# FFN weights in a two-layer hybrid block: down weights in quarters with slots of their own, up weights in turns over two pairs

## The chip, the cores and the metric

The kernel runs on one core of one Trainium2 chip. The metric is the device time of one execution in microseconds (us), the median of several runs; a lower one is better. The trace is one profiled execution of the same program. Engines are named PE (matrix products; PEld its weight loads), DVE, ACT, POOL and SP (SP issues nearly all transfers here).

## What is computed

A backbone of two layers over 1280 tokens (1024 latent and 256 context tokens) of 1024 features. Each layer has three groups of mixers (attention, mLSTM, Hyena), a shared output projection, and then the ConvFFN that this case is about; conditioning (adaLN) gives shift, scale and gate of each norm. The last layer needs only the 1024 latent tokens. The ConvFFN in the reference's terms, cut to what matters:

```python
D_FF = ((8 * D_MODEL // 3 + 255) // 256) * 256      # 2816
# u = norm2(x) @ w_up                 -> 2 * D_FF features: a half "a" and a half "b"
# u = dwconv(u, 3 taps along tokens)  -> each feature by itself
# g = silu(a) * b
# x = x + gate * (g @ w_down)         -> 1024 features
```

Products are wanted at fp32 accuracy, and the kernel makes each from three products of fp32r halves (hi by hi, hi by lo, lo by hi).

## The kernel before

**Tiles.** Features lie on the 128 partitions, tokens along the free axis, in blocks of 512, 512 and 256 tokens (the last layer has the first two only). The 2816 hidden features are 22 tiles. For one tile j and one half `ab` (0 for a, 1 for b) `up` computes `u`: 8 input tiles by 3 passes by the blocks, so 72 matmuls in layer 0 and 48 in layer 1, into the PSUM tile `u3` (printed as `u`). `conv` then takes `u` through ACT (L1525), DVE (L1526, L1527) and for ab = 0 ACT again (L1530); DVE multiplies the halves (L1551); `split` makes `g` hi on ACT (L290) and lo on DVE (L291).

**Pairs.** Tiles come in pairs (2p, 2p+1), 11 of them. The loop of `ffn` runs up of the even tile, then `down` of the pair before, then up of the odd tile. Below, ua0 and ub0 are the two up weights of the even tile, ua1 and ub1 those of the odd one. `down` makes, for each of 8 tiles of output features and each block, one piece: 6 matmuls (two j by three passes) into the PSUM tile `pj` or `pk` in turn, one buffer each, and DVE's L1576 adds the piece, times the gate, onto the residual stream `S`. A piece can so only start when L1576 has emptied the piece two before it. The down of the last pair stands behind the loop, with the blocks outermost, and feeds the next norm.

**Weights.** A raw weight tile `wr` (128x1024 fp32, 512 KB, two slots) comes by a transfer on SP's queue: one for each up weight (L295), one for each half of the output features of a pair's down weights (L1562). `wsplit` makes hi from it by an ACT cast (L307) and lo by a POOL subtraction (L308). The raw slot is free when both are through; the slots of hi and lo are free when the last matmul that reads them is through. In the FFN these 1024-wide slots are three pairs: two named `wh` and one named `wx`, which all weights, up and down, take in turn:

```python
self.wturn = (self.wturn + 1) % 3
if self.wturn == 0:
    p, tag = self.wx, "wx"
```

**Order.** A list scheduler of the framework gives each engine its order when the program is built, from dependences, slots and its own estimates; the engines then run their lists in order and wait for each other by semaphores. So the order of engines is known beforehand, and the rows of the section on the change are taken from it. SP's list too is in order: a transfer that waits for a slot holds all behind it.

**What else runs.** In layer 0 DVE also computes the adaLN rows of layer 1 in between (`ada_some`, L416, printed as CUSTOM_DVE_ANT_0 in the trace and as ISA in the order, each with a read of its accumulator behind it), 12 for each tile j, with weights `aw` that SP loads into three slots (L412).

Of the kernel before, what the change touches and what calls it, by code (L numbers as in the profile page):

```python
# [196 lines left out]
class Kern:  # L197
    def __init__(self, tc, a, out):
        self.tc, self.nc, self.a, self.out = tc, tc.nc, a, out
        self.n = self.turn = self.wturn = 0  # L200
        self.wx = self.adas = None
        self.wpool = False
        self.pools, self.fixed, self.events = [], 0, 0

# [90 lines left out]
        self.nc.sync.dma_start(wr[:, :cols], ap)  # L295
        return self.wsplit(wr[:, :cols], cols)

    def wsplit(self, wr, cols=1024):

        p, tag = self.wp, "wh"  # L300
        if self.wx is not None:
            self.wturn = (self.wturn + 1) % 3
            if self.wturn == 0:
                p, tag = self.wx, "wx"
        hi = self.t(p, [128, 1024], tag, F32R)[:, :cols]
        lo = self.t(p, [128, 1024], tag, F32R)[:, :cols]
        self.nc.scalar.copy(hi, wr)  # L307
        (self.nc.gpsimd if self.wpool else self.nc.vector).tensor_tensor(lo, wr, hi, op=ALU.subtract)  # L308
        return hi, lo
# [1191 lines left out]
    def ffn(self, L, xs, hs, rp, pp, between):  # L1501

        nc, a = self.nc, self.a
        last = L == DEPTH - 1
        blocks = [0, 1] if last else [0, 1, 2]
        W = 1024 if last else TP
        ffc = self.t(rp, [128, 44, 4], "ffc")
        nc.sync.dma_start(ffc, a["ffc"][L])

        def begin(j, ab):  # L1510
            return [j, ab, self.weight(a["wup"][L, j, ab]), self.t(pp, [128, 1024 if last else 1536], "u3")]

        def piece(u, b):
            wh, wl = u[2]
            t0 = BLK[b][0]
            for k in range(8):
                hi, lo = hs[k][b]
                self.mm3(u[3][:, t0:t0 + hi.shape[-1]], wh[:, 128 * k:128 * k + 128], wl[:, 128 * k:128 * k + 128],
                         hi, lo, k == 0, k == 7)

        def conv(u):
            j, ab, _, pu = u
            cw = ffc[:, j + N_FF * ab]
            y = self.t(rp, [128, TP], "sa")
            nc.scalar.activation(y[:, :W], pu[:, :W], AF.Identity, scale=cw[:, 1:2], bias=cw[:, 3:4])  # L1525
            nc.vector.scalar_tensor_tensor(y[:, 1:W], pu[:, 0:W - 1], cw[:, 0:1], y[:, 1:W], op0=ALU.mult, op1=ALU.add)  # L1526
            nc.vector.scalar_tensor_tensor(y[:, 0:W - 1], pu[:, 1:W], cw[:, 2:3], y[:, 0:W - 1], op0=ALU.mult, op1=ALU.add)  # L1527
            self.ada_some(pu, 3)
            if ab == 0:
                nc.scalar.activation(y[:, :W], y[:, :W], AF.Silu)  # L1530
            return y

        def up(j):
            if j == 0:
                us = [begin(j, ab) for ab in range(2)]
                for u in us:
                    piece(u, 0)
                ys = []
                for u in us:
                    for b in blocks[1:]:  # L1540
                        piece(u, b)
                    ys.append(conv(u))
            else:
                ys = []
                for ab in range(2):
                    u = begin(j, ab)
                    for b in blocks:
                        piece(u, b)
                    ys.append(conv(u))
            ya, yb = ys  # L1550
            nc.vector.tensor_tensor(yb[:, :W], ya[:, :W], yb[:, :W], op=ALU.mult)  # L1551
            self.ada_some(ya, 3)
            gh = self.t(rp, [128, TP], "g", F32R)
            gl = self.t(rp, [128, TP], "g", F32R)
            self.split(yb[:, :W], gh[:, :W], gl[:, :W])
            self.ada_some(yb, 3)
            return gh, gl

        def down_w(js, mh):

            wr = self.t(self.wp, [128, 1024], "wr")
            nc.sync.dma_start(wr.rearrange("p (j c) -> p j c", j=2),  # L1562
                              a["wdn"][L, js[0]:js[0] + 2, :, 512 * mh:512 * mh + 512].rearrange("j p c -> p j c"))
            hi, lo = self.wsplit(wr)
            return [(hi[:, 512 * i:512 * i + 512], lo[:, 512 * i:512 * i + 512]) for i in range(2)]

        def down_piece(gs, ws, m, b):
            t0, n, s = BLK[b]
            h0 = t0 + s
            ps = self.ps()[:, :n]  # L1570
            for i, ((gh, gl), (wh, wl)) in enumerate(zip(gs, ws)):
                o = 128 * (m % 4)
                self.mm3(ps, wh[:, o:o + 128], wl[:, o:o + 128], gh[:, h0:h0 + n], gl[:, h0:h0 + n],
                         i == 0, i == len(gs) - 1)
            x = xs[m][:, t0:t0 + n]
            nc.vector.scalar_tensor_tensor(x, ps, self.mods[L][:, 40 + m, s:s + 1], x, op0=ALU.mult, op1=ALU.add)  # L1576

        def down(js, gs):
            for mh in range(2):
                ws = down_w(js, mh)  # L1580
                for m in range(4 * mh, 4 * mh + 4):
                    for b in blocks:
                        down_piece(gs, ws, m, b)

        pend = None
        for p in range(N_FF // 2):
            g0 = up(2 * p)
            if pend is not None:
                down(*pend)
            g1 = up(2 * p + 1)  # L1590
            pend = ((2 * p, 2 * p + 1), (g0, g1))
        js, gs = pend
        accs = {}
        assert self.adas is None
        if not last:
            self.gain(L + 1, 0)
            self.gain(L + 1, 1, 1)
        self.wpool = WP
        for b in blocks:
            for mh in range(2):  # L1600
                ws = down_w(js, mh)
                for m in range(4 * mh, 4 * mh + 4):
                    down_piece(gs, ws, m, b)
                    accs[b] = self.square(accs.get(b), xs[m], b, rp, ("B", "B"), nc.gpsimd if BETA and b < 2 else None)
                    if m == MB and b:
                        between(b - 1, accs[b - 1])
        between(blocks[-1], accs[blocks[-1]])
        self.wpool = False
# [11 lines left out]
    def run(self):  # L1620
        nc, a = self.nc, self.a
        with ExitStack() as es:
# [46 lines left out]
            for L in range(DEPTH):  # L1669
# [22 lines left out]
                        assert self.adas is None  # L1692
                        self.gain(L, 1)
                with ExitStack() as e4:
                    rp = self.pool(e4, f"r5{L}", sa=2, g=6, wx=2, aw=3, rs_s=1, rs_r=1, rs_v=1, rs_d=1)
                    src = a["xT"] if L == 0 else self.xsp
                    nt = NX if last else T
                    xs = []
# [13 lines left out]
                    self.w_out(L, xs, groups, between_w)  # L1712
                    for b in groups[-1]:
                        norm2(b)
                    self.wx = rp
                    pp = self.pool(e4, f"p5{L}", PSUM, u3=3 if last else 2)
                    if not last:
                        self.hs = [{} for _ in range(8)]
# [15 lines left out]
                        self.ada_run(chain(self.ada_rows(1, range(16), (0, 1), *args),  # L1734
                                           self.ada_rows(1, range(16, 48), (0,), *args)))
                    self.ffn(L, xs, hs, rp, pp, between)
                    self.wx = None


# [15 lines left out]
```

## Time and profile before

| what | value |
|---|---|
| median of 3 runs | 3794.49 us (3793.99 to 3797.38) |
| profiled execution, its own time | 3789.71 us |
| its span in the trace | 3787.9 us |
| TensorE clock granted over the span | 0.955 of full |
| PE busy | 3491.6 us, 92% of the span |
| DVE / ACT / POOL busy | 2236.5 / 1283.6 / 942.8 us |
| FFN of layer 0, FFN of layer 1 in the trace | about 1119 to 2111 us, about 3005 to 3788 us |

The profiled execution lies 1.8 us above its own span and 4.8 us below the median of the runs. A "wait" in the trace is idle time of an engine just before an instruction, put down to the instruction that released it last. Matmuls are pipelined: a row's own duration is a little longer than its distance to the next one.

### The profile page before, as it was taken

Reading aid. Unit: us, or ns where it says so; the run is one execution under the profiler, and the core shown is the slowest. Engines: PE = TensorE matmul, PEld = TensorE weight load, DVE = VectorE, ACT = ScalarE, POOL = GpSimd, SP = SyncE. Lnnn points to the kernel's source line nnn. Section 1 sums busy time; section 2 is a strip of 40 time slices with the busy share of each in tenths; the row PEclk is TensorE's granted clock in tenths of the full one; section 3 lists DMA queues with packets and bytes.
Section 4 is the critical chain, followed back from the end, with each engine's and each line's share of the span. In section 5 each row is a group of like instructions: output and inputs, shape, how many; then the busy total and the mean of one; then the engine's idle time right before and its main releaser. Section 6 shows DMA issues by size and latency. Waiting matters only on the chain. (4 is left out here: it accounts for less than half of the span.)

```text
span 3787.9 us, 45575 instructions
## 1 busy us (share of the span) xinstructions
PE 3491.6 (92%) x16896; PEld 2780.0 (73%) x16896; DVE 2236.5 (59%) x3765; ACT 1283.6 (34%) x2069; POOL 942.8 (25%) x782
## 2 busy tenths in 40 slices
PE   5999978788888999999999899878999999999997
PEld 3798755566677888888887678766666778888875
DVE  5646678888765554555555765576665643434335
ACT  4433315454442211211212443325565322222222
POOL 1402443333301111111111141152433122222221
PEclk7999889899999999999999999989999999999998
DMA  5322532243431111122222232352222211111111
GB/s 180 113 69 91 199 122 85 83 116 98 128 114 59 53 63 56 55 78 73 74 81 74 83 108 78 115 168 70 65 81 80 90 45 49 47 50 45 45 51 67
DMA packets 190666, 322.09 MB, mean 85 GB/s; under 512 B 34003, under 2 KB 99108, under 8 KB 190444
## 3 DMA queue, kind: packets, MB, share of 16 engines
q1 hardware_dynamic: 189900, 318.87, 26.9%
q8 instruction: 133, 2.18, 0.2%
q14 instruction: 89, 0.73, 0.1%
q0 software_dynamic: 544, 0.31, 0.0%
HBM read 266.13 MB, written 52.81 MB: 84 GB/s over the span
## 5 line engine op out<-in xcount | busy, mean ns | idle before, releaser
L259 PE MATMUL u<-B,wh 128*128 128x512 f32 (+1 forms) x3240 | 729.0, 377 | 18.9 <-ACT wh L307 10.6
L259 PEld LDWEIGHTS u<-B,wh 128*128 128x128 f32 x3240 | 575.4, 189 | 143.3 <-ACT wh L307 12.7
L308 POOL TENSOR_TENSOR wh<-wr,wh 128x1024 fp32r<-128x1024 f32 x92 | 222.5, 2419 | 1115.3 <-ACT wh L307 1073.7
L259 PE MATMUL u<-B,wx 128*128 128x512 f32 (+1 forms) x2040 | 435.9, 368 | 8.6 <-DVE mods L416 8.6
L307 ACT CAST wh<-wr 128x1024 fp32r<-128x1024 f32 (+2 forms) x188 | 189.0, 1006 | 744.4 <-PE u L259 425.7
L259 PEld LDWEIGHTS u<-B,wx 128*128 128x128 f32 x2040 | 353.7, 189 | 77.3 <-issue 8.8
L259 PE MATMUL pj<-B,wh 128*128 128x512 f32 (+1 forms) x1644 | 382.3, 378 | 22.1 <-DVE wh L308 8.6
L259 PE MATMUL pk<-B,wh 128*128 128x512 f32 (+1 forms) x1485 | 354.7, 386 | 29.5 <-ACT S L645 7.4
L259 PEld LDWEIGHTS pj<-B,wh 128*128 128x128 f32 x1644 | 288.2, 193 | 89.6 <-issue 15.2
L259 PEld LDWEIGHTS pk<-B,wh 128*128 128x128 f32 x1485 | 266.5, 198 | 99.8 <-issue 13.3
L1401 POOL TENSOR_TENSOR Pl<-P,Ph 128x512 fp32r<-128x512 f32 (+1 forms) x168 | 236.1, 1408 | 372.3 <-ACT Ph L1400 315.0
L1576 DVE SCALAR_TENSOR_TENSOR S<-pk,mods,S 128x512 f32<-128x512 f32 (+1 forms) x220 | 152.6, 694 | 285.9 <-PE pk L259 285.7
L259 PE MATMUL st<-qh,S 96*128 96x512 f32 (+1 forms) x960 | 296.3, 417 | 21.3 <-DMA qh<-mr 17.4
L1576 DVE SCALAR_TENSOR_TENSOR S<-pj,mods,S 128x512 f32<-128x512 f32 (+1 forms) x220 | 152.7, 694 | 269.9 <-PE pj L259 269.8
L1365 DVE TENSOR_REDUCE mx<-sm 128x1 f32<-128x512 f32 (+1 forms) x400 | 228.0, 588 | 83.8 <-PE sm L259 81.4
L1526 DVE SCALAR_TENSOR_TENSOR sa<-u,ffc,sa 128x1281 f32<-128x1281 f32 (+1 forms) x88 | 124.4, 1413 | 235.1 <-ACT sa L1525 234.3
L1399 ACT ACTIVATE P<-st 128x512 f32<-128x512 f32 (+1 forms) x336 | 199.2, 594 | 180.0 <-PE st L259 99.6
L259 PE MATMUL pk<-g,wh 128*128 128x512 f32 (+1 forms) x1032 | 242.5, 370 | 7.8 <-ACT g L290 3.9
L259 PE MATMUL pj<-g,wh 128*128 128x512 f32 (+1 forms) x1032 | 245.6, 370 | 2.7 <-POOL wh L308 1.6
L259 PEld LDWEIGHTS st<-qh,S 96*128 96x128 f32 (+1 forms) x960 | 186.3, 200 | 78.7 <-DMA qh<-mr 21.8
L259 PE MATMUL pv<-Ph,B 128*64 128x512 f32 (+2 forms) x672 | 213.9, 400 | 9.7 <-ACT Ph L1400 9.5
L1400 ACT ACTIVATE Ph<-st 128x512 fp32r<-128x512 f32 (+1 forms) x336 | 198.7, 593 | 44.2 <-PE pv L259 16.7
(397 smaller groups left out, 5199.8 us busy)
## 6 DMA issues: line engine op xcount, KB each, us to landing
wr<-in_wup_dram SPq DMA_DIRECT2D x88, 512.0 KB
wr<-in_wdn_dram SPq DMA_DIRECT2D x50, 512.0 KB
aw<-in_adawT_dram SPq DMA_DIRECT2D x192, 128.0 KB
wr<-in_wout_dram SPq DMA_DIRECT2D x40, 512.0 KB
aw<-in_adawT_dram SPq DMA_DIRECT2D x64, 256.0 KB
wr<-in_win_dram SPq DMA_DIRECT2D x28, 512.0 KB
S<-in_xT_dram SPq DMA_DIRECT2D x16, 640.0 KB
mlrb<-rrows SPq DMA_DIRECT2D x36, 256.0 KB
```

What stands on the lines that cost most here:

```text
L259: self.nc.tensor.matmul(out, lhsT, rhs, start=start, stop=stop)
L307: self.nc.scalar.copy(hi, wr)
L308: (self.nc.gpsimd if self.wpool else self.nc.vector).tensor_tensor(lo, wr, hi, op=ALU.subtract)
L1365: nc.vector.reduce_max(st["mx"][:, qt, bi:bi + 1], ps[:, :kn], axis=AX.X)
L1399: nc.scalar.activation(P[:, :n], ps[:, :n], AF.Exp, scale=SCALE)
L1400: nc.scalar.activation(Ph[:, :n], ps[:, :n], AF.Exp, scale=SCALE)
L1401: (nc.gpsimd if j % 2 else nc.vector).tensor_tensor(Pl[:, :n], P[:, :n], Ph[:, :n], op=ALU.subtract)
L1526: nc.vector.scalar_tensor_tensor(y[:, 1:W], pu[:, 0:W - 1], cw[:, 0:1], y[:, 1:W], op0=ALU.mult, op1=ALU.add)
L1576: nc.vector.scalar_tensor_tensor(x, ps, self.mods[L][:, 40 + m, s:s + 1], x, op0=ALU.mult, op1=ALU.add)
```

## The change

Up weights now take turns in the two `wh` pairs alone. A pair's down weights come in quarters of 256 output features (two j, 128x512 for both, 256 KB) instead of halves, each through half of a raw slot `wr` and into slots `wd` of 512 columns; there are two pairs of these, in the space of the one `wx` pair. Below d0 to d3 are a pair's quarters (before: d0 and d1 its halves). A quarter serves 2 tiles of output features, so 6 pieces in layer 0 and 4 in layer 1; a half served 12 and 8. Matmuls, evacuations and bytes stay the same; down transfers, their casts and their subtractions are 100 each instead of 50, at half the size. Lines behind L307 move up by 5 (L1576 is L1571 in the changed kernel, L1526 is L1521, L1551 is L1546, L416 is L411, L1562 is L1557).

```diff
-    def wsplit(self, wr, cols=1024):
-
-        p, tag = self.wp, "wh"
-        if self.wx is not None:
-            self.wturn = (self.wturn + 1) % 3
-            if self.wturn == 0:
-                p, tag = self.wx, "wx"
-        hi = self.t(p, [128, 1024], tag, F32R)[:, :cols]
-        lo = self.t(p, [128, 1024], tag, F32R)[:, :cols]
+    def wsplit(self, wr, cols=1024, p=None, tag="wh", size=1024):
+
+        hi = self.t(p or self.wp, [128, size], tag, F32R)[:, :cols]
+        lo = self.t(p or self.wp, [128, size], tag, F32R)[:, :cols]
         self.nc.scalar.copy(hi, wr)
         (self.nc.gpsimd if self.wpool else self.nc.vector).tensor_tensor(lo, wr, hi, op=ALU.subtract)
...
-        def down_w(js, mh):
-
-            wr = self.t(self.wp, [128, 1024], "wr")
+        def down_w(js, mq):
+
+            wr = self.t(self.wp, [128, 1024], "wr")[:, :512]
             nc.sync.dma_start(wr.rearrange("p (j c) -> p j c", j=2),
-                              a["wdn"][L, js[0]:js[0] + 2, :, 512 * mh:512 * mh + 512].rearrange("j p c -> p j c"))
-            hi, lo = self.wsplit(wr)
-            return [(hi[:, 512 * i:512 * i + 512], lo[:, 512 * i:512 * i + 512]) for i in range(2)]
+                              a["wdn"][L, js[0]:js[0] + 2, :, 256 * mq:256 * mq + 256].rearrange("j p c -> p j c"))
+            hi, lo = self.wsplit(wr, 512, rp, "wd", 512)
+            return [(hi[:, 256 * i:256 * i + 256], lo[:, 256 * i:256 * i + 256]) for i in range(2)]
...
-            for mh in range(2):
-                ws = down_w(js, mh)
-                for m in range(4 * mh, 4 * mh + 4):
+            for mq in range(4):
+                ws = down_w(js, mq)
+                for m in range(2 * mq, 2 * mq + 2):
...
-                    rp = self.pool(e4, f"r5{L}", sa=2, g=6, wx=2, aw=3, rs_s=1, rs_r=1, rs_v=1, rs_d=1)
+                    rp = self.pool(e4, f"r5{L}", sa=2, g=6, wd=4, aw=3, rs_s=1, rs_r=1, rs_v=1, rs_d=1)
...
-                    self.wx = rp
```

The engines' orders are the same up to the FFN of layer 0. Three places show how the rest moves; names carry the buffer's number at their end, so that `wr_11831` is one raw tile.

SP's list for one pair in layer 0, before: the two halves d0 and d1 (`in_wdn_dram`), then ua1, ub1 and the next ua0 (`in_wup_dram`), with adaLN weights `aw` between them.

```order
L1562 DMA wr_11603<-in_wdn_dram 128x2x512
L1562 DMA wr_11705<-in_wdn_dram 128x2x512
L412 DMA aw_11393<-in_adawT_dram 128x256
L295 DMA wr_11807<-in_wup_dram 128x1024
L412 DMA aw_11401<-in_adawT_dram 128x256
L412 DMA aw_11405<-in_adawT_dram 128x256
L412 DMA aw_11492<-in_adawT_dram 128x256
L412 DMA aw_11580<-in_adawT_dram 128x256
L295 DMA wr_11896<-in_wup_dram 128x1024
L412 DMA aw_11584<-in_adawT_dram 128x256
L295 DMA wr_12005<-in_wup_dram 128x1024
```

The same pair in the changed kernel (d0, `wr_11615`, stands two rows ahead of the first row here): d1, d2, d3, then ua1 (`wr_11831`).

```order
L1557 DMA wr_11669<-in_wdn_dram 128x2x256
L1557 DMA wr_11723<-in_wdn_dram 128x2x256
L1557 DMA wr_11777<-in_wdn_dram 128x2x256
L407 DMA aw_11405<-in_adawT_dram 128x256
L407 DMA aw_11413<-in_adawT_dram 128x256
L407 DMA aw_11417<-in_adawT_dram 128x256
L407 DMA aw_11504<-in_adawT_dram 128x256
L407 DMA aw_11592<-in_adawT_dram 128x256
L407 DMA aw_11596<-in_adawT_dram 128x256
L407 DMA aw_11601<-in_adawT_dram 128x256
L295 DMA wr_11831<-in_wup_dram 128x1024
```

With two raw slots, ua1's load, which was third in the turn of the raw tiles from d0 on, is now fifth: it takes the slot of d2.

PE's list where `down` of that pair begins, before: behind the first two pieces (12 matmuls, the last two are the first rows here) the first two matmuls of ua1 (`u`), then the third piece, then 24 matmuls of ua1 (the last three rows are their first).

```order
L259 MATMUL pj_11617<-g_11397,wh_11605 128x512
L259 MATMUL pj_11617<-g_11396,wh_11606 128x512
L259 MATMUL u_2688_11813<-B_9766,wx_11809 128x512
L259 MATMUL u_2688_11813<-B_9767,wx_11809 128x512
L259 MATMUL pk_11625<-g_10996,wh_11605 128x256
L259 MATMUL pk_11625<-g_10997,wh_11605 128x256
L259 MATMUL pk_11625<-g_10996,wh_11606 128x256
L259 MATMUL pk_11625<-g_11396,wh_11605 128x256
L259 MATMUL pk_11625<-g_11397,wh_11605 128x256
L259 MATMUL pk_11625<-g_11396,wh_11606 128x256
L259 MATMUL u_2688_11813<-B_9766,wx_11810 128x512
L259 MATMUL u_2688_11813<-B_9772,wx_11809 128x512
```

The first matmuls of ua1 in the changed kernel; ahead of them stand all 6 pieces of d0 and 3 of d1 without a matmul of ua1 between (the first row here is the last matmul of the ninth piece).

```order
L259 MATMUL pk_11691<-g_11408,wd_11672 128x256
L259 MATMUL u_2700_11837<-B_9766,wh_11833 128x512
L259 MATMUL u_2700_11837<-B_9767,wh_11833 128x512
L259 MATMUL pj_11699<-g_10996,wd_11671 128x512
L259 MATMUL pj_11699<-g_10997,wd_11671 128x512
```

So ua1 begins after nine pieces instead of two. All ten pairs of layer 0 have this order, and the ten of layer 1 also have nine pieces ahead of ua1.

DVE's list of the changed kernel in that stretch (`aw` in a row marks adaLN; the row with `g_11605` is L291; the evacuation of the fifth piece stands first, those of the seventh to ninth at the end):

```order
L1571 SCALAR_TENSOR_TENSOR S_9233<-pk_11653,mods_14_194,S_9233 128x512
L411 ISA u_2652_11514,mods_19_202<-aw_11592,rs_d_10409,mods_19_202 128x256
...
L1571 SCALAR_TENSOR_TENSOR S_9233<-pj_11661,mods_14_194,S_9233 128x256
L411 ISA sa_11498,mods_19_202<-aw_11596,rs_d_10409,mods_19_202 128x256
...
L411 ISA u_2652_11514,mods_19_202<-aw_11592,adarow_10410,mods_19_202 128x256
...
L291 TENSOR_TENSOR g_11605<-sa_11587,g_11604 128x1282
L411 ISA sa_11498,mods_19_202<-aw_11596,adarow_10410,mods_19_202 128x256
...
L1571 SCALAR_TENSOR_TENSOR S_9235<-pk_11675,mods_14_194,S_9235 128x512
L1571 SCALAR_TENSOR_TENSOR S_9235<-pj_11683,mods_14_194,S_9235 128x512
```

Ahead of these rows DVE has, in this order: the evacuation of piece 1, L1521 of ub0, the evacuations of pieces 2 and 3, L1522, the evacuation of piece 4, one adaLN row, and L1546. The ninth evacuation comes behind two further adaLN rows.

## Rows read from the trace of the kernel before

**Rows 1.** Page, share of each engine and granted clock in 40 slices

```profile
PE 3491.6 (92%) x16896; PEld 2780.0 (73%) x16896; DVE 2236.5 (59%) x3765; ACT 1283.6 (34%) x2069; POOL 942.8 (25%) x782
```

**Rows 2.** Windows of the two FFNs: pairs and tails, busy time by engine

```profile
1250.00:1900.00 650.00, 641.53 (x3287) 543.30 (x3287) 343.94 (x632) 126.92 (x106) 110.62 (x46) 1.00 0.21 65
...
3100.00:3700.00 600.00, 598.36 (x2572) 481.78 (x2571) 241.16 (x251) 133.42 (x126) 130.00 (x54) 1.00 0.16 48
```

**Rows 3.** Waits of PE, 1119 to 2135 us: total, times, longest

```profile
PE u L259 <- ACT wh L307: 10.6, 10, 1.1
...
PE pk L259 <- ACT g L290: 3.9, 1, 3.9
```

**Rows 4.** Waits of PE, 2997 to 3788 us: total, times, longest

```profile
PE u L259 <- DVE sa L1527: 3.8, 1, 3.8
...
PE pj L259 <- POOL wh L308: 1.6, 9, 0.2
PE pj L259 <- ACT g L290: 1.4, 1, 1.4
```

**Rows 5.** Timeline of one pair of layer 0: start, duration, engine, line

```profile
1345.89 1.56 PE L259 MATMUL pj<-g,wh 128*128 128x512 f32 x6
...
1347.28 1.55 PE L259 MATMUL pk<-g,wh 128*128 128x512 f32 x6
1347.48 0.75 DVE L1576 SCALAR_TENSOR_TENSOR S<-pj,mods,S 128x512 f32<-128x512 f32 x1 [1.03 <-PE pj L259]
...
1348.67 0.89 PE L259 MATMUL pj<-g,wh 128*128 128x256 f32 x6
1349.52 1.04 ACT L307 CAST wh<-wr 128x1024 fp32r<-128x1024 f32 x1 [1.96 <-PE pj L259]
...
1350.62 0.73 PE L259 MATMUL u<-B,wh 128*128 128x512 f32 x2 [1.06 <-ACT wh L307]
1350.64 2.42 POOL L308 TENSOR_TENSOR wh<-wr,wh 128x1024 fp32r<-128x1024 f32 x1 [25.63 <-ACT wh L307]
...
1352.24 1.11 DVE L416 CUSTOM_DVE_ANT_0 u<-aw,rs_d,mods 128x256 f32<-128x256 f32 x1
...
1353.08 0.33 SPq L295 DMA_DIRECT2D wr<-in_wup_dram  x1
...
1355.00 0.48 DVE L416 CUSTOM_DVE_ANT_0 u<-aw,rs_d,mods 128x256 f32<-128x256 f32 x1
1355.40 0.14 DVE L416 DVE_READ_ACCUMULATOR2_ANT mods<- 128x1 f32 x1
...
1356.89 1.05 ACT L307 CAST wx<-wr 128x1024 fp32r<-128x1024 f32 x1 [3.32 <-DMA wr<-in_wup_dram]
```

**Rows 6.** Groups of DVE by shape, 1250 to 1900 us

```profile
L1526 DVE SCALAR_TENSOR_TENSOR sa<-u,ffc,sa 128x1281 f32<-128x1281 f32 x30 | 46.4, 1547 | 27.7 <-ACT sa L1525 27.0
...
L1551 DVE TENSOR_TENSOR sa<-sa,sa 128x1282 f32<-128x1282 f32 x15 | 22.3, 1487 | 0.0
L291 DVE TENSOR_TENSOR g<-sa,g 128x1282 fp32r<-128x1282 f32 x14 | 20.9, 1490 | 0.0
...
L1576 DVE SCALAR_TENSOR_TENSOR S<-pk,mods,S 128x256 f32<-128x256 f32 x31 | 15.0, 482 | 48.2 <-PE pk L259 48.2
```

**Rows 7.** Groups of ACT by shape, whole run: a cast of 512 columns

```profile
L660 ACT CAST lh<-S 128x512 fp32r<-128x512 f32 x20 | 12.3, 619 | 16.3 <-DVE S L657 13.2 <-DVE sn_k L523 1.6 <-DMA cq<-lh 1.3
```

**Rows 8.** Groups of POOL by shape, whole run: subtractions of 512 and 1024 columns

```profile
L1401 POOL TENSOR_TENSOR Pl<-P,Ph 128x512 fp32r<-128x512 f32 x160 | 229.5, 1437 | 354.8 <-ACT Ph L1400 304.5 <-PE pv L259 26.4 <-PE sm L259 12.4
L308 POOL TENSOR_TENSOR wh<-wr,wh 128x1024 fp32r<-128x1024 f32 x92 | 222.5, 2419 | 1115.3 <-ACT wh L307 1073.7 <-PE u L259 30.4 <-DMA aw<-in_adawT_dram 11.2
```

**Rows 9.** Groups of DVE by shape, 3100 to 3700 us

```profile
L1526 DVE SCALAR_TENSOR_TENSOR sa<-u,ffc,sa 128x1023 f32<-128x1023 f32 x36 | 46.0, 1278 | 145.5 <-ACT sa L1525 145.5
```

**Rows 10.** Timeline of layer 0's tail behind the last up matmul

```profile
2068.86 0.50 PE L259 MATMUL pk<-g,wh 128*128 128x512 f32 x1 [3.90 <-ACT g L290]
...
2072.45 2.93 PE L259 MATMUL pk<-g,wh 128*128 128x512 f32 x6
```

More of the change, by code (lines that the diff above doesn't have):

```diff
@@ L200, in __init__ @@
         self.n = self.turn = self.wturn = 0
-        self.wx = self.adas = None
+        self.adas = None
         self.wpool = False
@@ L1571, in down_piece @@
             for i, ((gh, gl), (wh, wl)) in enumerate(zip(gs, ws)):
-                o = 128 * (m % 4)
+                o = 128 * (m % 2)
                 self.mm3(ps, wh[:, o:o + 128], wl[:, o:o + 128], gh[:, h0:h0 + n], gl[:, h0:h0 + n],
@@ L1599, in ffn @@
         for b in blocks:
-            for mh in range(2):
-                ws = down_w(js, mh)
-                for m in range(4 * mh, 4 * mh + 4):
+            for mq in range(4):
+                ws = down_w(js, mq)
+                for m in range(2 * mq, 2 * mq + 2):
                     down_piece(gs, ws, m, b)
@@ L1736, in run @@
                     self.ffn(L, xs, hs, rp, pp, between)
-                    self.wx = None
 def kernel(**inputs):
```

## The prediction

> **What bounds the kernel now.** I read the page's shares first: PE is busy for 3491.6 of 3787.9 us, DVE for 2236.5, POOL for 942.8 [rows 1]. PE is the bound, and what the change costs or gives is idle time of PE. Next the windows: in the pairs of layer 0 PE is busy for 641.53 of 650 us, in those of layer 1 for 598.36 of 600 [rows 2]. So the FFN has next to nothing left to win, and much to lose. Then the waits of PE. Layer 0 has one that comes back: ten times 1.06 us, 10.6 in all, for the cast of an up weight [rows 3]. Layer 1 has nothing of the kind; its largest that repeats is 1.6 us in nine times for a POOL subtraction, and 1.6 us idle in the 600, which are nine pairs, make about 0.2 per pair [rows 2, 4].
>
> The timeline shows where the 1.06 comes from [rows 5]. d0's last piece ends, ACT casts at 1349.52 (1.04) into the slot that d0 held, and PE's first `u` of ub1 starts at 1350.62. POOL subtracts until 1353.06, SP issues the next raw load at 1353.08, and the cast of that tile (an `in_wup` load of 512 KB) starts at 1356.89. From issue to cast takes 3.81 us. These are the prices of the chain that the change lengthens.
>
> **The change, part by part.** *Removed*: the wait for a slot that d0 held. Up weights no longer queue behind down weights for `wh`, so the ten waits of 1.06 us go: -10.6 us at most.
>
> *Added work*: 50 transfers, 50 casts and 50 subtractions more, at half size. A cast of 512 columns takes 0.62 us [rows 7]; a subtraction of 512 takes between 1.21 (half of 2.42) and 1.44 us [rows 8], I take 1.25. ACT and POOL are idle for most of the FFN (126.92 and 110.62 busy in 650 [rows 2]), so 100 casts at 0.62 against 50 at 1.05 cost nothing by themselves. For the load of a quarter the trace of before has no row. It is bounded above by the 3.81 of a tile of twice the bytes, below by 1.9, half of it; d2 and d3 are loaded long ahead, so neither end moves the sum outside the tails.
>
> *Moved, first chain*: ua1's raw load. There are two raw slots, and d2 and d3 sit in both, because their splits need the `wd` pairs that d0 and d1 hold. So ua1's load waits until d2 is split, d2's split until d0's last matmul. Take t = 0 at d0's first matmul. d0 has four pieces of 512 at 1.39 us (1345.89 to 1347.28) and two of 256 at half of that [rows 5]: 7.0 us if nothing holds them. Then cast 0.62, subtraction 1.25, load 3.81, cast 1.05 and some hops of 0.05: PE can start ua1 at 13.9. The work that stands in PE's list ahead of it is nine pieces, six of 512 and three of 256: 10.5 us. That alone leaves 3.4 us idle, once per pair. Before, ua1's tile was loaded during the up stage, and PE had its matmuls to mix in from the third piece on.
>
> *Moved, second chain*: evacuations. Two PSUM buffers, so piece i+2 waits for L1576 of piece i. As long as PE mixes `u` in, DVE has time; with nine pieces back to back, DVE must keep up while it also has ub0's convolution, L1551, L291 and adaLN rows in its list. I walk the list with the trace's durations: L1526 and L1527 1.55, L1551 and L291 1.49, L1576 0.75 and 0.48 [rows 6], an adaLN row 0.48 and 0.14 for its accumulator; L1576 starts 1.59 after its piece [rows 5].
> - Evacuation 1 ends at 2.34, L1526 at 3.89, evacuation 2 at 4.64. Piece 3 runs in between, piece 4 starts at 4.70 instead of 3.50: 1.2 us idle.
> - Evacuation 3 ends at 5.05, L1527 at 6.60, evacuation 4 at 7.35, an adaLN row and L1551 at 9.35, evacuation 5 at 10.1. Piece 6 starts at 7.48 and d0 is done at 8.2; piece 7 starts at 10.15: 1.95 idle.
> - Then evacuation 6, three adaLN rows, L291 and a fourth row: evacuation 7 ends at 15.05. Piece 8 runs from 11.54, piece 9 starts at 15.1: 2.2 idle. ua1 starts at 15.8.
>
> In this walk ua1's cast is done by 15.15 (d0 done at 8.2, and the chain above), so the two chains end nearly together and don't add. PE's idle time per pair is 5.3 us against 1.06 now: +4.2. The other bound is the first chain alone: 3.4, so +2.3. I take +3.6 per pair, nearer to the walk, since it follows the engine's real list, but below it, since it uses no slack anywhere. Ten pairs: **+36 us** (23 to 42). Behind ua1's start nothing is late: ub1's tile has some 14 us of ua1's matmuls to come in, and the next pair's tiles a whole up stage.
>
> *Layer 1* has no adaLN rows, and its L1526 takes 1.28 [rows 9]. The same walk gives gaps of 0.7 (piece 3), 0.5 (piece 6) and nothing behind, so ua1 starts at 13.7 where nine pieces are 12.5; ua1's cast ends at 13.1, in time. Idle 1.2 against 0.2: +1.0 per pair by the walk, 0 where DVE's order has slack. I take **+7 us** for ten pairs (0 to 10).
>
> *Ends.* In layer 0's tail PE waits 3.9 us for `g` [rows 10]. The pieces of the pair before, some of which now cover a part of that chain, stand earlier in the changed list, so I add 1.4 us, one piece uncovered; behind it a quarter gives 2.8 us of matmuls in a block of 512 against 1.9 for a split, which is enough, and 1.4 in the block of 256, which isn't. Together +2.5 (0 to 5). Layer 1's tail loses the same cover around its wait of 1.4: +2.5 (0 to 5). Its start mixes two up tiles instead of three, which saves part of the 3.8 wait [rows 4] but waits for a cast and a subtraction instead: +0.5. Ends: **+5.5 us** (0 to 10).
>
> Sum: 36 + 7 + 5.5 = +48.5 on the profiled execution's 3789.7, so 3838; on the median of the runs, which lies 4.8 above it, 3843. I forecast **3841 us**.
>
> **A rule beside the rows.** An adaLN row that starts at 1352.24, while POOL subtracts, takes 1.11 us, and one at 1355.00, after it, 0.48 [rows 5]. That a subtraction delays a DVE row that is not L1576 is thus in the trace. The Trainium skill (SBUF — State Buffer, section "Who interferes with whom") says that a DVE instruction with two inputs in SBUF and a GpSimd instruction that reads SBUF exclude each other for a whole instruction, whichever starts first; the row agrees for one direction, and no row that I read shows POOL held by DVE. By that rule L1551, which runs until 9.35 in the walk, could hold d2's subtraction, due at about 8.9, and the later load of ua1; an estimate by that page is ua1 half a microsecond later in each pair. What it would do as a mechanism of this kernel is rival 3.
>
> **The rivals.**
> 1. *The first chain alone.* DVE gets through in time, as in layer 1. Idle 3.4 in layer 0, ends and layer 1 at their low values: +23 to +30, 3812 to 3826. For it: half of DVE's time in the pairs is idle (343.94 busy of 650 [rows 2]). Against it: the engine's list puts the long rows between the evacuations.
> 2. *The clock falls in the gaps.* In layer 0's tail six matmuls take 2.93 us at 2072.45 [rows 10] against 1.56 in a pair [rows 5], behind a wait of 3.90 us. If two pieces in each pair of layer 0 went at that pace, 2 x 1.37 x 10 = +27 on top: 3868. For it: the walk's gaps add up to 5.3 us in 16. Against it: none is over 2.2 by itself.
> 3. *Subtraction and DVE rows hold each other.* If d2's subtraction waits for a whole L1551 (1.49 [rows 6]), ua1 starts at up to 16.6 instead of 15.8: +8, so 3849. It counts only where L1551 begins just ahead of the subtraction.
> 4. *Only the gain.* The ten waits go and nothing replaces them: 3794.5 - 10.6 = 3784, faster. It decides by one point: ua1's tile must be cast within 10.5 us of d0's start, so its load issued by 5.6 (10.5 less 3.81 and 1.05). d0 isn't done before 7.0, and d2's split comes behind it, so this needs a raw slot that d2 doesn't hold. The list shows none.
> 5. *No difference.* New gaps of just the size of the old one, 1.06 per pair in layer 0, and nothing in layer 1: 3794.5. It needs the load of 3.81 to shrink to about 1.5.
>
> **How the numbers follow.** Forecast by the walk, 3826 to 3857: 0.58. Rival 1: 0.15. Rival 2: 0.11. Rival 3: 0.06. Rival 4: 0.05. Rival 5: 0.05. The range takes in the forecast and rivals 1 to 3: from 3812 (23 and nothing else, on the profiled execution) to 3868. About 0.2% (8 us) is what a measurement of this kernel can tell from no change. Slower 0.90, same 0.05, faster 0.05.
>
> **What would show it.** In the changed kernel's trace: ten times, in layer 0, nine pieces with waits for DVE's L1571 before the fourth, seventh and ninth, of 1 to 2 us each, or instead one wait of 1 to 3 us for ua1's cast at `u`; SP's load of ua1 issued right behind d2's subtraction, some 10 us after d0's first matmul; and the first cast of ua1 some 3.8 us later. PE busy in a window of layer 0's pairs should fall from 98.7% to about 94%, that of layer 1 by about 1%. I am wrong if ua1's load goes out before d0 ends, if PE has other `u` matmuls between the nine pieces, or if the clock in those windows falls below 1.00.

## The result and the profile after

The changed kernel takes 3853.35 us (median of 4 runs, 3846.98 to 3854.69) against 3794.24 for the kernel before (4 runs, 3790.76 to 3797.38): a ratio of 1.0146, 95% interval 1.0124 to 1.0168. It is slower by 59 us by the medians and by 55 (47 to 64) by the ratio, where 3841 was forecast. Its profiled execution took 3852.89 us with a span of 3851.1, and the mean granted clock is 0.955, as before.

The windows of the pairs in the two layers, with the columns of [rows 2]:

```profile
1250.00:1900.00 650.00, 615.04 (x3096) 513.63 (x3097) 335.76 (x615) 123.05 (x116) 110.65 (x60) 0.99 0.20 64
...
3100.00:3700.00 600.00, 595.50 (x2556) 477.56 (x2555) 235.23 (x249) 138.48 (x145) 130.39 (x71) 1.00 0.15 47
```

PE was busy for 641.53 of 650 us in layer 0 and is now for 615.04; in layer 1 it went from 598.36 to 595.50 of 600. The granted clock is 1.00 in three of these four windows and 0.99 in layer 0's of the changed kernel, which has two short stretches below full speed (see rival 2 below). So the loss is nearly all stops of PE, and next to none of it matmuls at a lower clock. What PE waited for, in layer 0's FFN and its tail (the view of [rows 3], here from 1100 to 2200 us):

```profile
PE pk L259 <- DVE S L1571: 32.8, 27, 1.6
PE pj L259 <- DVE S L1571: 11.8, 13, 2.1
...
PE pk L259 <- ACT g L290: 6.5, 1, 6.5
PE u L259 <- ACT wh L302: 5.6, 5, 1.4
```

and in layer 1's (the view of [rows 4], here from 2990 to 3852 us):

```profile
PE pj L259 <- DVE S L1571: 6.5, 13, 0.5
PE pj L259 <- ACT g L290: 4.9, 1, 4.9
...
PE u L259 <- POOL wh L303: 1.7, 1, 1.7
```

The ten equal waits of 1.06 us are gone. Some 40 waits for L1571, which empties PSUM for the next piece, stand in their place, 35 of them in the ten pairs; the last five pairs have one more each, for the cast of ua1's tile (the 5.6 us).

One pair of layer 0, from its first down piece on, answers to [rows 5]. These are the pieces that PE started late, the first matmuls of ua1, and, to compare, three rows of pieces:

```profile
1335.18 1.66 PE L259 MATMUL pj<-g,wd 128*128 128x512 f32 x6 [0.85 <-DVE S L1571]
...
1338.06 0.88 PE L259 MATMUL pj<-g,wd 128*128 128x256 f32 x6
1340.15 1.66 PE L259 MATMUL pk<-g,wd 128*128 128x512 f32 x6 [1.22 <-DVE S L1571]
...
1344.91 0.99 PE L259 MATMUL pk<-g,wd 128*128 128x256 f32 x6 [1.62 <-DVE S L1571]
1345.74 0.62 PE L259 MATMUL u<-B,wh 128*128 128x512 f32 x2
...
1348.83 1.66 PE L259 MATMUL pk<-g,wd 128*128 128x512 f32 x6 [1.08 <-DVE S L1571]
...
1354.29 0.87 PE L259 MATMUL pj<-g,wd 128*128 128x256 f32 x6
1355.00 1.54 PE L259 MATMUL pk<-g,wd 128*128 128x512 f32 x6
```

The late ones are the 4th, 7th, 9th and 11th piece; d0's first matmul is at 1330.67. Each stop costs more than its wait. The piece ahead of it takes its whole 0.88 (1338.06), where the next piece begins 0.71 after the start when PE goes on (1354.29, 1355.00); and the piece that was late is followed after 1.49 us instead of 1.39. Together that is some 0.28 for each stop: PE is busy for 85.17 us in this pair of 89.93 us, and for 84.04 in a pair of the first experiment below, which has no stop, so 1.13 for four stops. The chain of ua1's tile in the same pair, with the DVE rows that matter:

```profile
1338.90 0.62 ACT L302 CAST wd<-wr 128x512 fp32r<-128x512 f32 x1 [6.61 <-PE pj L259]
...
1339.60 1.29 POOL L303 TENSOR_TENSOR wd<-wr,wd 128x512 fp32r<-128x512 f32 x1 [33.31 <-ACT wd L302]
...
1340.91 0.33 SPq L295 DMA_DIRECT2D wr<-in_wup_dram  x1
...
1344.11 0.74 DVE L1571 SCALAR_TENSOR_TENSOR S<-pk,mods,S 128x512 f32<-128x512 f32 x1
1344.16 1.05 ACT L302 CAST wh<-wr 128x1024 fp32r<-128x1024 f32 x1 [3.42 <-DMA wr<-in_wup_dram]
...
1345.29 2.39 POOL L303 TENSOR_TENSOR wh<-wr,wh 128x1024 fp32r<-128x1024 f32 x1 [4.40 <-ACT wh L302]
1345.43 2.53 DVE L411 CUSTOM_DVE_ANT_0 sa<-aw,adarow,mods 128x256 f32<-128x256 f32 x1
```

d2's cast begins when d0's last matmul ends, SP issues ua1's load 0.02 us after d2's subtraction (at 10.24 from d0's start), and the cast follows 3.25 us later. Its end, 1345.21, and that of the evacuation the ninth piece waits for, 1344.85, lie 0.4 us apart: both chains of the prediction end together. In the last five pairs the evacuation comes first: the ninth piece waits for 1.22 us only, and PE then waits 1.01 to 1.35 us for ua1's cast, while the wait before the 11th piece is gone. The last row is an adaLN row that takes 2.53 us instead of some 0.48, beside ua1's subtraction.

From one pair to the next (9 periods, by the first wait of each) it takes 90.12 us now, (2056.19 - 1245.11) / 9, against 85.43 before, (2034.01 - 1265.17) / 9. In layer 1, from the first piece of one pair to that of the next, it takes 67.64 us now, (3748.77 - 3139.99) / 9, against 67.24 before, (3689.28 - 3151.38) / 8.

| stretch of the trace | before | after | difference |
|---|---|---|---|
| FFN of layer 0: first up matmul to first matmul of the next layer | 976.7 | 1024.9 | +48.3 |
| of that, ten pairs | | | +46.9 |
| FFN of layer 1: first up matmul to the last rstd matmul | 771.3 | 776.7 | +5.5 |
| of that, ten pairs | | | +4.0 |

The FFNs hold 53.7 of the spans' difference of 63.2 us. The rest lies in front of the first FFN (1134.87 against 1139.55, where both kernels have the same lists) and in layer 1's mixers.

### The profile page after: what moved, and what is told of

Its sections match the earlier page's. It is cut to its first block, busy times and chain, and to the rows that moved or that the text cites. A ratio compares the mean times of both kernels' runs of the same rounds, so it can differ in the third digit from the quotient of the medians.

```text
span 3851.1 us, 45878 instructions
## 1 busy us (share of the span) xinstructions
PE 3502.7 (91%) x16896; PEld 2780.4 (72%) x16896; DVE 2228.8 (58%) x3765; ACT 1292.4 (34%) x2119; POOL 952.1 (25%) x832
## 5 line engine op out<-in xcount | busy, mean ns | idle before, releaser
L259 PE MATMUL u<-B,wh 128*128 128x512 f32 (+1 forms) x5280 | 1144.0, 373 | 20.9 <-DVE mods L411 8.6
L259 PEld LDWEIGHTS u<-B,wh 128*128 128x128 f32 x5280 | 925.3, 189 | 211.4 <-issue 8.8
L303 POOL TENSOR_TENSOR wh<-wr,wh 128x1024 fp32r<-128x1024 f32 x88 | 212.6, 2416 | 635.4 <-ACT wh L302 619.9
L259 PE MATMUL pk<-g,wd 128*128 128x512 f32 (+1 forms) x1320 | 321.2, 378 | 40.7 <-DVE S L1571 33.0
L303 POOL TENSOR_TENSOR wd<-wr,wd 128x512 fp32r<-128x512 f32 x100 | 132.3, 1323 | 906.9 <-ACT wd L302 906.9
L259 PEld LDWEIGHTS pj<-B,wh 128*128 128x128 f32 x1644 | 288.1, 193 | 90.1 <-issue 15.8
L259 PE MATMUL pj<-g,wd 128*128 128x512 f32 (+1 forms) x1320 | 322.6, 380 | 23.5 <-DVE S L1571 18.3
L1521 DVE SCALAR_TENSOR_TENSOR sa<-u,ffc,sa 128x1281 f32<-128x1281 f32 (+1 forms) x88 | 124.6, 1416 | 375.7 <-ACT sa L1520 375.6
L259 PEld LDWEIGHTS pk<-g,wd 128*128 128x128 f32 x1320 | 232.7, 190 | 102.1 <-DVE S L1571 46.6
L1571 DVE SCALAR_TENSOR_TENSOR S<-pk,mods,S 128x512 f32<-128x512 f32 (+1 forms) x220 | 152.5, 693 | 256.3 <-PE pk L259 256.1
L259 PEld LDWEIGHTS pj<-g,wd 128*128 128x128 f32 x1320 | 234.4, 191 | 82.3 <-DVE S L1571 28.4
L1571 DVE SCALAR_TENSOR_TENSOR S<-pj,mods,S 128x512 f32<-128x512 f32 (+1 forms) x220 | 152.6, 694 | 232.6 <-PE pj L259 232.3
```

The costliest lines, as they stand in the source:

```text
L259: self.nc.tensor.matmul(out, lhsT, rhs, start=start, stop=stop)
```

## The experiments

Eight kernels in two groups; each group has its own runs of the kernel before (median 3805.0 in the first, 3803.6 in the second), so the ratios are compared, not the times.

### ua1 ahead of d2

```diff
...
             if pend is not None:
-                down(*pend)
-            g1 = up(2 * p + 1)
+                down(*pend, (0, 1))
+                ua = begin(2 * p + 1, 0)
+                down(*pend, (2, 3))
+            g1 = up(2 * p + 1, ua)
...
```

(`down` makes the quarters that it is given, and `up` takes the half that is already begun)

> The changed kernel, but the weight of the odd tile's first half (ua1) is begun between d1 and d2, so that its raw load takes the slot of d0 and not that of d2. Theory A (ua1's raw load behind d2's split makes PE run nine pieces back to back): PE's list mixes ua1 in from the third piece on, the waits for L1571 in the pairs go, a pair of layer 0 takes 84.3 to 85.4 us instead of 89.9, and the time is 3785 to 3800, at or a little below the kernel before. Theory B (quarters themselves cost: more transfers, casts, subtractions, DVE too slow for them): a pair stays above 88 us and the time above 3835.

Measured: ratio 0.9915 (0.9903 to 0.9928), 3775.86 us where the kernel before took 3804.96. Quarters, slots, casts, subtractions and transfers are those of the changed kernel; only the raw tile's turn moved. The same windows as above:

```profile
1250.00:1900.00 650.00, 650.00 (x3335) 551.70 (x3334) 364.05 (x655) 127.92 (x122) 120.55 (x62) 1.00 0.22 68
3100.00:3700.00 600.00, 600.00 (x2589) 485.88 (x2588) 235.91 (x253) 137.04 (x144) 141.95 (x72) 1.00 0.15 47
```

PE never stops there. In the pairs two pieces stand ahead of ua1 and then up matmuls between nearly all:

```profile
1330.97 1.55 PE L259 MATMUL pk<-g,wd 128*128 128x512 f32 x6
1332.36 1.54 PE L259 MATMUL pj<-g,wd 128*128 128x512 f32 x6
1333.74 4.12 PE L259 MATMUL u<-B,wh 128*128 128x512 f32 x17
...
1415.01 1.55 PE L259 MATMUL pk<-g,wd 128*128 128x512 f32 x6
```

A pair takes 84.04 us, so the changed kernel loses 6.1 in each and the kernel before 1.4. Theory B falls: quarters as such cost PE nothing. I had not expected the size of the gain: FFN 0 took 956.9 us, 19.8 below before, and FFN 1 764.9, 6.3 below. Of the 19.8, the pairs are 13.9. The rest lies outside the pairs, for the most part in the tails: half of the pieces of the loop's last `down` (those of d2 and d3) now stand behind ua1 in the list and are left over for the wait for `g`, which is in the list of waits no more (3.9 and 1.4 us before, 6.5 and 4.9 in the changed kernel). That the rest is wholly this wait I didn't test by itself.

### Halves again, in a pair of their own

```diff
...
-                              a["wdn"][L, js[0]:js[0] + 2, :, 256 * mq:256 * mq + 256].rearrange("j p c -> p j c"))
-            hi, lo = self.wsplit(wr, 512, rp, "wd", 512)
+                              a["wdn"][L, js[0]:js[0] + 2, :, 512 * mq:512 * mq + 512].rearrange("j p c -> p j c"))
+            hi, lo = self.wsplit(wr, 1024, rp, "wd", 1024)
...
-                    rp = self.pool(e4, f"r5{L}", sa=2, g=6, wd=4, aw=3, rs_s=1, rs_r=1, rs_v=1, rs_d=1)
+                    rp = self.pool(e4, f"r5{L}", sa=2, g=6, wd=2, aw=3, rs_s=1, rs_r=1, rs_v=1, rs_d=1)
```

> Half of the change undone: down weights come in halves of 512 output features again, but in one pair of slots of their own, and up weights keep to their two pairs. Raw tiles are d0, d1, ua1, ub1 again, so ua1 takes the slot of d0. Theory A: like the kernel before or a little better, 3785 to 3800. Theory C (up weights with two pairs instead of three is what costs): like the changed kernel, 3840 or more. d1 now has to wait for d0's last matmul; theory A expects that ub1's matmuls cover its cast and subtraction, or else one wait of 1 to 3 us per pair.

Measured: ratio 1.0046 (1.0032 to 1.006), 3824 us. Neither theory's time. The pairs of layer 0 do what theory A says (85.21 us from 1329.12 to 1414.33, PE busy 643.43 of 650), and those of layer 1 keep PE busy for 600.00 of 600 us, so two pairs for up weights are enough. The loss is outside the pairs, 18 us in FFN 0 and 8 in FFN 1 (994.8 and 779.3 us). In layer 0's tail, one pair of slots leaves each half's split bare:

```profile
2073.66 0.73 PE L259 MATMUL pk<-g,wd 128*128 128x512 f32 x2 [1.81 <-ACT wd L302]
...
2076.46 2.07 PE L259 MATMUL pk<-g,wd 128*128 128x512 f32 x4 [1.60 <-POOL wd L303]
...
2085.17 0.73 PE L259 MATMUL pk<-g,wd 128*128 128x512 f32 x2 [1.06 <-ACT wd L302]
...
2087.78 1.21 PE L259 MATMUL pk<-g,wd 128*128 128x512 f32 x4 [1.41 <-POOL wd L303]
```

Five waits for a cast and three for a subtraction stand in that tail, and the clock granted from 2090 to 2138 us is 0.79, that is, part of it at the lower level of 1.2 GHz. I had looked at the pairs alone. This is where quarters are worth something: with two pairs of slots the changed kernel has no such wait.

### adaLN rows ahead of the FFN

```diff
+                    if not last:
+                        sc = self.t(pp, [128, 1536], "u3")
+                        while self.adas is not None:
+                            self.ada_some(sc, 12)
                     self.ffn(L, xs, hs, rp, pp, between)
```

The changed kernel and the kernel before, each with this edit (`sc` is a scratch tile). Each ran once; only the length of a pair is read.

> The changed kernel with all adaLN rows of layer 1 worked off before the first up matmul of layer 0's FFN, so that DVE has none in the pairs; the total is longer by that block, only the pairs' period is read (against the kernel before with the same move, next). Theory A1 (two chains that end together: ua1's late tile alone leaves some 3.4 us): the period stays 2 to 3 us above that of the next kernel, and the wait is put down to ua1's cast instead of L1571. Theory A2 (evacuations alone): the period is within 0.7 us of the next kernel's.

> The kernel before with the adaLN rows worked off ahead of the FFN. All theories: one wait of about 1.06 us for ub1's cast in each pair as now, since that wait hangs on d0's slot and not on DVE: a period of 85.2 to 85.5 us.

The changed kernel so:

```profile
1795.04 1.66 PE L259 MATMUL pj<-g,wd 128*128 128x512 f32 x6 [0.85 <-DVE S L1571]
...
1799.61 1.66 PE L259 MATMUL pk<-g,wd 128*128 128x512 f32 x6 [0.81 <-DVE S L1571]
...
1802.82 0.98 PE L259 MATMUL pk<-g,wd 128*128 128x256 f32 x6 [0.17 <-DVE S L1571]
...
1807.99 4.45 PE L259 MATMUL u<-B,wh 128*128 128x512 f32 x18 [0.22 <-POOL wh L303]
...
1882.15 1.66 PE L259 MATMUL pj<-g,wd 128*128 128x512 f32 x6 [0.85 <-DVE S L1571]
```

and the kernel before:

```profile
1725.12 0.73 PE L259 MATMUL u<-B,wh 128*128 128x512 f32 x2 [1.06 <-ACT wh L307]
...
1810.56 0.73 PE L259 MATMUL u<-B,wh 128*128 128x512 f32 x2 [1.06 <-ACT wh L307]
```

Periods of 87.11 and 85.44: 1.7 apart, between both forms of the theory, and none of the waits is put down to ua1's cast (the 0.22 of the fourth row is for its subtraction). In one pair of that run the cast ends 15.05 us after d0's first matmul, as late as ever, but the scheduler has now eleven pieces ahead of ua1 instead of nine, 2.8 us more work. So the late tile is no floor of 3.4 us: further pieces can fill it. The waits that are left, 0.85, 0.81 and 0.17, are for L1571 of the pieces beside ub0's convolution, for which there are two PSUM buffers as before.

### The same adaLN rows, but not beside the nine pieces

```diff
-            self.ada_some(pu, 3)
+            self.ada_some(pu, 3 if j == 0 or ab == 0 and j % 2 == 0 else 5 if j % 2 else 0)
...
-            self.ada_some(ya, 3)
+            self.ada_some(ya, 3 if j == 0 else 5 if j % 2 else 0)
...
-            self.ada_some(yb, 3)
+            self.ada_some(yb, 3 if j == 0 else 6 if j % 2 else 0)
```

> The changed kernel with the same adaLN rows, but none in the stretch in which nine pieces run back to back: those of the even tile's second half, its product and its split are worked off in the odd tile. Theory A (evacuations queue behind adaLN rows in DVE's list): the waits before the seventh, ninth and eleventh piece shrink to 0.8, 0.2 and nothing, a pair takes about 87.2 us instead of 89.9, the time is some 27 us below the changed kernel, a ratio to the kernel before of 1.007 to 1.009. Rival E (ua1's late tile sets the pair): the waits move to ua1's cast, a pair stays at 89 or more, ratio 1.012 or more.

Measured: ratio 1.0092 (1.0076 to 1.0109), just above the 1.007 to 1.009 that theory A gave.

```profile
1608.77 1.67 PE L259 MATMUL pj<-g,wd 128*128 128x512 f32 x6 [1.41 <-DVE S L1571]
...
1613.34 1.66 PE L259 MATMUL pk<-g,wd 128*128 128x512 f32 x6 [0.79 <-DVE S L1571]
...
1616.57 0.99 PE L259 MATMUL pk<-g,wd 128*128 128x256 f32 x6 [0.17 <-DVE S L1571]
...
1695.91 1.66 PE L259 MATMUL pj<-g,wd 128*128 128x512 f32 x6 [0.85 <-DVE S L1571]
```

The waits before the 7th and 9th piece shrink from 1.22 and 1.62 to 0.79 and 0.17, and the one before the 11th is gone; the one before the 4th is 1.41 in the first five pairs and 0.85 in the others. A pair takes 87.28 us, (2043.69 - 1258.15) / 9, so the edit is worth 2.8 of the 6.1 us that a pair loses, and what rival E said would happen did not. But the edit moved PE's list too: as with the adaLN rows ahead, eleven pieces stand ahead of ua1 and not nine. In the sixth pair ua1's cast ends at 1706.29, 14.9 us after d0's first matmul, and the tenth piece starts at 1704.52. With nine pieces ahead PE would have waited some 1.8 us there (an estimate from these two times). So this run does not part the place of the adaLN rows from the two pieces more, and ua1's late tile is covered rather than shown to be harmless.

### POOL's large subtraction in two

```diff
+        if self.wpool and cols == 1024:
+            for c in (slice(0, 512), slice(512, 1024)):
+                self.nc.gpsimd.tensor_tensor(lo[:, c], wr[:, c], hi[:, c], op=ALU.subtract)
+            return hi, lo
```

(lines behind it move down by 4 against the changed kernel: L415 is L411, L386 is L382)

> The changed kernel with POOL's subtraction of 1024 columns cut into two of 512. Theory F (the adaLN row of 2.53 us beside ua1's subtraction waits for a lock that POOL holds for a whole instruction): the longest adaLN rows in the pairs fall to 1.2 to 1.7 us, the wait before the eleventh piece shrinks by about a microsecond, a pair takes 88.6 to 89.2 us, the time is some 10 us below the changed kernel (ratio 1.011 to 1.014). Rival: the row is long for its own weights or data, and stays at 2.4 to 2.6 us. If the second half takes the lock before DVE does, rows of 2.5 stay too, and the run doesn't tell.

Measured: ratio 1.0128 (1.0109 to 1.0146): 7 us below the changed kernel by the ratios, with intervals that overlap, so the time alone doesn't tell. On the row's length the rows do:

```profile
1616.23 2.58 POOL L305 TENSOR_TENSOR wh<-wr,wh 128x512 fp32r<-128x512 f32 x2 [4.83 <-ACT wh L302]
...
1617.52 1.57 DVE L415 CUSTOM_DVE_ANT_0 sa<-aw,rs_d,adab 128x256 f32<-128x256 f32 x1
```

The longest adaLN row of the pairs falls from 2.62 (2.53 in the pair shown above) to 1.57; this one stands beside the second half alone and ends at 1619.09, 0.28 behind it, just as the one of 2.53 ended at 1347.96, 0.28 behind a subtraction that ended at 1347.68. In the first five pairs the wait before the 11th piece is gone, and the pair from 1605.68 to 1694.30 takes 88.62 instead of about 90. That this is the shorter hold is not shown, since PE's list moved too: 12 up matmuls instead of none stand before the 11th piece. In the pair shown the two halves held two DVE rows one after the other (L386 ahead of this one took 1.24 us, and 0.16 in the changed kernel), and the ninth evacuation came 17.85 us after d0's first matmul, no earlier than the 17.82 of the same pair of the changed kernel; in the third pair it came a microsecond earlier (16.62 against 17.61). In the last five pairs PE waits 1.03 to 1.25 us for ua1's cast, as in the changed kernel; over all ten a pair takes 89.25 us.

### The change in layer 1 alone

```diff
...
+                    rp = self.pool(e4, f"r5{L}", sa=2, g=6, **({"wd": 4} if last else {"wx": 2}), aw=3, rs_s=1, rs_r=1, rs_v=1, rs_d=1)
...
+                    self.wx = None if last else rp
```

(with `down_w` in quarters where `last` holds, and in halves elsewhere)

> The change made in layer 1 alone; layer 0 keeps the three turning pairs and halves. Theory A (nine tenths of the loss is layer 0's pairs): the FFN of layer 1 takes 776 to 778 us instead of 771, the time is 4 to 7 us above the kernel before, a ratio of 1.001 to 1.002. Rival D (the 5 us of the measured difference that the two FFNs' stretches don't hold are layer 1's): 10 us or more, 1.0027.

Measured: ratio 1.0019 (1.0007 to 1.003), +7 us by the ratio (3 to 11); FFN 1 took 776.1 us, 4.9 above before. Its row of waits is that of the changed kernel (6.4 us in 13 times against 6.5 in 13). Theory A holds for the FFN. Rival D isn't shown: the mixers of layer 1 were some 6 us longer in this trace (838.2 against 831.9 us to the last attention matmul), but up to there the lists of PE, DVE and ACT are the same as in the kernel before. In all ten traces that stretch takes 831.0 to 842.1 us, and the longest is that of the kernel before with the adaLN rows moved, whose layer 1 is untouched; so this is spread between executions. The first up matmul of layer 0's FFN, with the same lists ahead of it, comes between 1134.9 and 1153.7 us in the eight traces without that move.

### The kernel before with ua1 between d0 and d1

```diff
...
-                down(*pend)
-            g1 = up(2 * p + 1)
+                down(*pend, (0,))
+                ua = begin(2 * p + 1, 0)
+                down(*pend, (1,))
+            g1 = up(2 * p + 1, ua)
...
```

> The kernel before, halves and three turning pairs as they were, but ua1's weight is begun between d0 and d1, as the first experiment had it between d1 and d2. Theory G (that gain came from the order: ua1 early, and down pieces left over to cover the wait for g in the tails): ratio 0.990 to 0.995, about as the first experiment. Theory H (quarters in slots of their own were needed for it): a wait for ub1's slot stays in each pair (85.4 us), and only the tails gain, ratio 0.996 to 0.999.

Measured: ratio 0.9949 (0.9934 to 0.9964), 3781.66 us. PE is busy for 650.00 of 650 us in the pairs here too, so theory H falls for the pairs: the wait for ub1's slot went without any slot of its own, and a pair takes 84.09 us, (1919.28 - 1246.58) / 8, as in the first experiment (84.06 over nine). But the tails' wait stayed (3.9 us for `g` in layer 0, 4.7 in layer 1), and the gain is less than that of the first experiment, whose interval lies wholly below. So order gives most of the gain, and quarters with slots of their own some further 0.3%, of which the trace accounts for 5.4 us in the FFNs (960.7 and 766.5 us here), outside layer 0's pairs. That first experiment is the best version of all that ran.

## Why the prediction was right, point by point

- **What bounds the kernel.** Right: PE, with next to nothing to win in the pairs; the first experiment shows the most there is, 1.4 us per pair.
- **The wait removed.** Right: -10.6, the ten waits are gone. Each was worth 1.4, not 1.06 (85.43 against 84.04 us for a pair), since a stop costs more than its wait.
- **Casts, subtractions and transfers cost nothing by themselves.** Right: the first experiment has them all and PE busy for the whole window. d2's cast took 0.62 and its subtraction 1.29, as estimated.
- **First chain.** Right in its course: d0 done at 8.1 us, the load issued at 10.24, the cast ended at 14.5 from d0's start (15.15 by the sum; the load took 3.25 instead of 3.81). Wrong as a bound: with eleven pieces ahead of ua1 (adaLN rows ahead) the chain is as late and costs less. In the last five pairs it is what PE waits for: SP stands at `aw` transfers, issues ua1's load 0.8 us late (1792.29 instead of 1791.53), and PE waits 1.01 to 1.35 for the cast. That comes in the place of the wait before the 11th piece, not on top of it.
- **Second chain.** Right in its places, the 4th, 7th and 9th piece. The walk gave 1.2, 1.95 and 2.2 us, measured are 0.85, 1.22 and 1.62, and ua1 starts 15.07 us after d0's first matmul instead of 15.8. It didn't see the 11th, 1.08, ahead of which an adaLN row is held by ua1's subtraction in the pair shown.
- **Layer 0's pairs, +36 (23 to 42).** Too small; it measured +46.9, 4.7 per pair against 3.6. This is the term that was mis-sized. The waits themselves came out: over nine pairs PE is idle for 4.62 us in each, against 1.06 before, so +3.56. That is partly luck, since three waits shorter than in the walk and a fourth that it didn't have make up for each other; the discount "since it uses no slack anywhere" was due. What has no term in the sum is what a stop costs besides its wait: PE's busy time rose from 84.37 to 85.50 us per pair. 0.8 of these 1.1 us are three stops more at 0.28, the rest is the clock (rival 2).
- **Layer 1's pairs, +7 (0 to 10).** +4.0: one gap of 0.5 instead of two.
- **Ends, +5.5.** +2.9 in the two FFNs together; the waits for `g` grew as forecast (3.9 to 6.5 and 1.4 to 4.9), but others went: at layer 1's start 3.8 gave way to 0.5 and 1.7, and in its tail the last down weights' cast and subtraction (0.9 and 1.3) are waited for no more.
- **Rival 2, the clock.** Seen in little: two pairs show it in the window of 0.99, and by its letter the prediction's own sign of being wrong (below 1.00) is met. In the sixth pair, after PE's fourth stop, the clock granted from 1705 to 1710 us is 0.66, so part of it is at the lower level of 1.2 GHz, and the next piece takes 2.43 us instead of 1.55:

```profile
1706.38 1.22 PE L259 MATMUL u<-B,wh 128*128 128x512 f32 x2 [1.02 <-ACT wh L302]
1707.40 2.43 PE L259 MATMUL pj<-g,wd 128*128 128x512 f32 x6
```

  PE is busy for 86.50 and 86.76 us in the sixth and seventh pair against 85.14 to 85.25 in the seven others, so it costs 1.3 to 1.6 us in each of the two and not 2.7 in every pair. The tenth pair shows a third such stretch (0.89 from 2060 to 2070 us).
- **Rival 3.** It did not come up at d2: its subtraction started 0.08 us behind its cast, after L1546 had ended at 1339.44. But a subtraction that waits for DVE is in the traces: in the first experiment one subtraction of 512 columns in each pair takes 2.1 us instead of 1.29; the one at 1317.01 starts inside L291 (1316.44, 1.50 us). PE doesn't wait for it. In the changed kernel it is the other direction that shows beside the late pieces. The Trainium skill (SBUF — State Buffer, section "Who interferes with whom") says that a DVE instruction with two inputs in SBUF waits for a whole GpSimd instruction that reads SBUF, and that one with at most one such input, outside the two-port perf modes, doesn't. The traces agree: adaLN rows take 2.53 beside 1024 columns and 1.57 beside 512, while L1571, whose other input is in PSUM, keeps its length. In the seventh pair one of each starts inside the same subtraction:

```profile
1797.24 2.49 POOL L303 TENSOR_TENSOR wh<-wr,wh 128x1024 fp32r<-128x1024 f32 x1 [5.71 <-ACT wh L302]
...
1797.42 0.48 DVE L1571 SCALAR_TENSOR_TENSOR S<-pk,mods,S 128x256 f32<-128x256 f32 x1
...
1797.89 2.13 DVE L411 CUSTOM_DVE_ANT_0 sa<-aw,rs_d,mods 128x256 f32<-128x256 f32 x1
```

- **The sum.** 48.5 forecast, 53.7 in the FFNs of the trace, 55 (47 to 64) by the ratio of the runs and 59 by the medians. The sum is nearer than its terms: 11 us too little in layer 0's pairs, 3 too much in layer 1's and 3 at the ends. What lies between the trace's 53.7 and the 59 is within the interval and within the spread of the mixers. A slip in rival 1 changes nothing else: its +30 gives 3820 on the profiled execution or 3824 on the median, not 3826.
- **What stays open.** That ua1's place in the turn of the raw tiles causes the loss is shown by the first experiment, which gives the whole of it back with quarters and slots as they are. How the loss of a pair is split between late evacuations and ua1's late tile is read from the trace, and no experiment parts the two: each that moved the adaLN rows moved PE's list as well.

## What to carry to other kernels

When tiles of one ring of raw slots serve two consumers, count the place of each load in the ring: a piece of work that is cut finer takes more turns, and the load behind it becomes as late as the last of them. Look then at what the scheduler puts in its place, since back-to-back pieces with two PSUM buffers run at the pace of the evacuating engine's whole list (here 4.7 us more per pair). Price each stop of PE above its wait, too. When such a change loses, try the order before the slots: here one moved line turned +1.5% into -0.85%.

## What the hardware showed that I had not expected

- Each stop of PE for an evacuation costs some 0.28 us beyond the wait that the trace shows: 0.17 ahead of it (a piece takes its whole 0.88 us instead of 0.71) and 0.11 behind it (1.49 instead of 1.39 us to the next piece). The trace counts these as busy time of PE.
- A 128x256 adaLN row of 0.48 us took 2.53 beside a POOL subtraction, and its end followed the end of that subtraction by 0.28 us, also when the subtraction was half as long. The other way round, a subtraction of 1.29 us took 2.09 where it started inside a long DVE row.
- The same program part, the mixers of layer 0, took between 1134.9 and 1153.7 us to the first up matmul in eight profiled executions (not all on the same chip), a spread of 0.5% of the whole; two kernels that differ by less than that in a trace have to be compared by stretches.
